# Rotary embedding on one core: tables first, one queue for loads and stores, 2 MB slabs, small first and last pieces, -sin on ScalarE

## Chip, cores, metric

The kernel runs on one NeuronCore of one Trainium2 chip. The metric is the device time of one execution in microseconds (us). "Span" is the length of the profiled execution; it is 1.7 to 1.8 us shorter than the time of the same run.

## The reference

`x` is float32 of shape 8 x 2048 x 8 x 64 (batch, sequence, heads, head size), 33.5 MB; `cos` and `sin` are 2048 x 32, 256 KB each.

```python
def reference(x, cos, sin):
    x1 = x[..., :32]; x2 = x[..., 32:]
    cos = cos[None, :, None, :]; sin = sin[None, :, None, :]
    out1 = x1 * cos - x2 * sin
    out2 = x1 * sin + x2 * cos
    return np.concatenate([out1, out2], axis=-1)
```

Every element is read once and written once, so at least 67 MB move. There are four multiplies and two adds for each pair, all elementwise.

## The kernel before

Each of the 128 partitions holds 16 neighbouring rows of the sequence of every batch, so a partition's data of one batch is 32 KB of contiguous memory. A tile is 4 of these rows (1 MB, 8 KB in each partition); there are 32 tiles and 20 buffers. GpSimd makes the sine products (`t2`), VectorE the cosine product (`t1`, in PSUM) and the sum. Loads are issued on the sync queue, stores and both tables on the ACT queue.

```python
    nc.scalar.dma_start(out=sin_sb, in_=sin_src)
    nc.scalar.dma_start(out=cos_sb, in_=cos_src)
    tiles = [(b, l) for l in range(n_blk) for b in range(B)]
    for i, (b, l) in enumerate(tiles):                      # 32 loads of 1 MB
        xt = xpool.tile([P, FREE], f32, tag="xt", name=f"xt{i}")
        nc.sync.dma_start(out=xt, in_=xv[b, :, l * FREE : (l + 1) * FREE])
        xts.append(xt)
    nc.vector.tensor_scalar_mul(ssin[:, :, 0, :], sin_sb, -1.0)   # -sin, sin
    nc.vector.tensor_copy(ssin[:, :, 1, :], sin_sb)
    nc.vector.tensor_copy(cos_ps, cos_sb)                         # cos to PSUM
    for i, (b, l) in enumerate(tiles):
        # ... (cut: tiles t1 in PSUM, t2 in SBUF, views)
        for u in range(2):
            nc.gpsimd.tensor_mul(out=..., in0=..., in1=rep(ssin[..., u, :], H))
        nc.vector.tensor_mul(out=t1..., in0=xt..., in1=rep(cos_ps[...], 2 * H))
        nc.vector.tensor_add(out=xt, in0=t1, in1=t2)
        nc.scalar.dma_start(out=ov[b, :, l * FREE : (l + 1) * FREE], in_=xt)
```

## Time and profile before

| | before |
|---|---|
| time, median | 168.08 us (3 runs, 168.06 to 168.24) |
| span | 166.6 us |
| VectorE / GpSimd busy | 148.2 / 146.3 us |
| bytes moved | 67.65 MB |
| first work on VectorE's tiles | 10.64 us |
| last add ends | 161.8 us |

From the page of the kernel before: the span, the busy times, the bytes per second in 40 equal slices of the span (4.2 us each), and the chain that ended last, by engine and by line.

```profile
span 166.6 us, 381 instructions
...
DVE 148.2 (89%) x67; POOL 146.3 (88%) x68
...
GB/s 167 424 428 421 374 431 423 433 427 425 431 421 431 429 427 427 425 433 419 433 425 423 433 419 433 423 433 427 425 431 421 431 427 427 429 423 433 285 220 252
...
DVE 89%; DMA 5%; issue 2%; DVEq 0%; ACTq 0%
DVE t L78 44%; DVE xt L83 44%; DMA cos_sb<-in_cos_dram 5%; DVE cos_ps L60 0%; DVEq L83 0%; ACTq L48 0%
```

Three things are nearly level: VectorE and GpSimd are busy for 88 to 89%, and the DMA moves 420 to 430 GB/s in nearly every slice. But the chain names VectorE for 89%, and the rest is the wait for the cosine table at the head; after the first slice and a dip to 374 in the fifth, the DMA slows down only in the last three slices, where it waits for VectorE.

From the timeline of the kernel before (columns: start, duration, engine, line, operation, what it writes and reads, shapes; in brackets the idle time of the engine before it and what ended it):

```profile
6.75 0.43 DVE L58 TENSOR_SCALAR ssin<-sin_sb 128x512 f32<-128x512 f32 x1 [6.75 <-DMA sin_sb<-in_sin_dram]
...
7.25 22.99 POOL L73 TENSOR_TENSOR t<-xt,ssin 128x1024 f32<-128x1024 f32 x10 [6.81 <-DVE ssin L58]
9.91 0.69 DVE L60 COPY cos_ps<-cos_sb 128x512 f32<-128x512 f32 x1 [2.41 <-DMA cos_sb<-in_cos_dram]
10.64 2.29 DVE L78 TENSOR_TENSOR t<-xt,cos_ps 128x2048 f32<-128x2048 f32 x1
13.04 2.29 DVE L83 TENSOR_TENSOR xt<-t,t 128x2048 f32<-128x2048 f32 x1
...
159.52 2.29 DVE L83 TENSOR_TENSOR xt<-t,t 128x2048 f32<-128x2048 f32 x1
```

The tables land at 6.75 and 9.91 us, VectorE begins its tiles at 10.64 and ends at 161.8: 32 pairs of multiply and add at 4.725 us, with no gap. GpSimd, with 64 operations between 7.25 and 153.4, needs 4.57 us a tile: a little faster than VectorE, and it starts 3.4 us ahead.

From the windows of the kernel before (columns: window, its length, VectorE's busy time and operations, GpSimd's the same, granted clock, busy share of the DMA engines, GB/s):

```profile
8.00:60.00 52.00, 48.67 (x22) 52.00 (x24) 1.00 1.01 423
60.00:120.00 60.00, 58.21 (x27) 60.00 (x27) 1.00 1.01 427
...
156.00:160.00 4.00, 3.86 (x3) 0.00 (x0) 1.00 0.70 289
160.00:162.00 2.00, 1.81 (x1) 0.00 (x0) 1.00 0.17 70
162.00:166.00 4.00, 0.00 (x0) 0.00 (x0) 1.00 0.64 262
```

The DMA is saturated (share about 1.0) at 423 to 427 GB/s, and after 156 us it has pauses: it waits for tiles. The tail, from the last add to the end, is 4.8 us and holds a 1 MB store.

### The profile page before, as it was taken

To read this page: it belongs to the slowest core of one execution; us is meant where nothing else is said; L and a number is where in the kernel's file an instruction comes from. 1 tells how busy PE (TensorE), PEld (TensorE's weight loads), DVE (VectorE), ACT (ScalarE), POOL (GpSimd) and SP (SyncE) were. 2 spreads that over 40 slices of the span, in tenths; PEclk is the share of its full clock that TensorE was granted. 3 is DMA by queue.
4 is the path that set the end of the run, shared out by engine and by line. 5 is a ranking of instruction groups with operands and counts; after the bars stand their busy time and mean duration, and the time that the engine had idled before them with its cause. 6 is when DMAs were issued, how large, how long until landed. Compare 5 with 4: busy or idle time off the path is not lost.

```text
span 166.6 us, 381 instructions
## 1 busy us (share of the span) xinstructions
DVE 148.2 (89%) x67; POOL 146.3 (88%) x68
## 2 busy tenths in 40 slices
DVE  0169999999999999999999999999999999999980
POOL 0299999999999999999999999999999999998000
DMA  5999999999999999999999999999999999999656
GB/s 167 424 428 421 374 431 423 433 427 425 431 421 431 429 427 427 425 433 419 433 425 423 433 419 433 423 433 427 425 431 421 431 427 427 429 423 433 285 220 252
DMA packets 9506, 67.65 MB, mean 406 GB/s; under 512 B 1056, under 2 KB 1056, under 8 KB 1312
## 3 DMA queue, kind: packets, MB, share of 16 engines
q10 hardware_dynamic: 4896, 34.08, 48.6%
q1 hardware_dynamic: 4608, 33.56, 48.3%
q14 instruction: 2, 0.02, 0.0%
HBM read 34.08 MB, written 33.55 MB: 406 GB/s over the span
## 4 chain that ended last, share of the span: by engine, by line
DVE 89%; DMA 5%; issue 2%; DVEq 0%; ACTq 0%
DVE t L78 44%; DVE xt L83 44%; DMA cos_sb<-in_cos_dram 5%; DVE cos_ps L60 0%; DVEq L83 0%; ACTq L48 0%
## 5 line engine op out<-in xcount | busy, mean ns | idle before, releaser
L73 POOL TENSOR_TENSOR t<-xt,ssin 128x1024 f32<-128x1024 f32 x64 | 146.1, 2341 | 6.8 <-DVE ssin L58 6.8
L83 DVE TENSOR_TENSOR xt<-t,t 128x2048 f32<-128x2048 f32 x32 | 73.3, 2291 | 3.3
L78 DVE TENSOR_TENSOR t<-xt,cos_ps 128x2048 f32<-128x2048 f32 x32 | 73.5, 2296 | 1.1
L58 DVE TENSOR_SCALAR ssin<-sin_sb 128x512 f32<-128x512 f32 x1 | 0.4, 426 | 6.7 <-DMA sin_sb<-in_sin_dram 6.7
L60 DVE COPY cos_ps<-cos_sb 128x512 f32<-128x512 f32 x1 | 0.7, 694 | 2.4 <-DMA cos_sb<-in_cos_dram 2.4
L59 DVE COPY ssin<-sin_sb 128x512 f32<-128x512 f32 x1 | 0.4, 419 | 0.0
L99 POOL MEMSET const-float32-0.0<- 128x1 f32 x1 | 0.1, 98 | 0.2 <-issue 0.2
L99 POOL MEMSET const-bfloat16-1.0<- 128x1 bf16 x1 | 0.1, 101 | 0.0
L99 POOL MEMSET const-uint8-127<- 128x1 uint8 x1 | 0.1, 101 | 0.0
L99 POOL MEMSET const-float32-1.0<- 128x1 f32 x1 | 0.1, 98 | 0.0
## 6 DMA issues: line engine op xcount, KB each, us to landing
xt<-in_x_dram SPq DMA_DIRECT2D x32, 1024.0 KB, 20.6
out_dram<-xt ACTq DMA_DIRECT2D x32, 1024.0 KB, 10.7
sin_sb<-in_sin_dram ACTq DMA_DIRECT2D x1, 256.0 KB, 6.0
cos_sb<-in_cos_dram ACTq DMA_DIRECT2D x1, 256.0 KB, 8.7
```

Source lines behind the costliest of these rows:

```text
L58: nc.vector.tensor_scalar_mul(ssin[:, :, 0, :], sin_sb, -1.0)
L59: nc.vector.tensor_copy(ssin[:, :, 1, :], sin_sb)
L60: nc.vector.tensor_copy(cos_ps, cos_sb)
L73: nc.gpsimd.tensor_mul(out=dst.rearrange("p (r h) d -> p r h d", h=H), in0=src.rearrange("p (r h) d -> p r h d", h=H), in1=rep(ssin[:, l * ...
L78: nc.vector.tensor_mul(out=t1.rearrange("p (r k d) -> p r k d", r=SL, d=Dh), in0=xt.rearrange("p (r k d) -> p r k d", r=SL, d=Dh), in1=rep ...
L83: nc.vector.tensor_add(out=xt, in0=t1, in1=t2)
L99: nc = _bacc.Bacc("TRN2", target_bir_lowering=False, num_devices=1)
```

## The change

The intent: start earlier (tables first, small first pieces, -sin made by ScalarE, which is idle), end sooner (small last pieces), and let loads and stores run in one orderly queue with large transfers: ten slabs of 2 MB are read ahead, then stores and loads alternate. The diff, cut to its core:

```diff
-    SL = 4                      # 32 tiles of 1 MB, 20 buffers
+    SL = 8                      # 16 slabs of 2 MB, 10 buffers
+    SLAB = SL * HD; UNIT = 4 * HD; NBUF = 10     # UNIT is 1 MB, HD is 256 KB
-    nc.scalar.dma_start(out=sin_sb, in_=sin_src)
+    def cuts(i):                # loads of slab i
+        if i == 0: return [HD, HD, 2 * HD, UNIT]
+        return [SLAB]
+    def pieces(i):              # computation
+        if i == 0: return [HD, HD, 2 * HD, UNIT]
+        if i == last: return [UNIT, 2 * HD, HD, HD]
+        return [UNIT, UNIT]
+    def stores(i): return pieces(i) if i == last else [SLAB]
+    nc.sync.dma_start(out=sin_sb, in_=sin_src)
     nc.scalar.dma_start(out=cos_sb, in_=cos_src)
+    for i in range(NBUF): load(i)                # all on the sync queue
-    nc.vector.tensor_scalar_mul(ssin[:, :, 0, :], sin_sb, -1.0)
-    nc.vector.tensor_copy(ssin[:, :, 1, :], sin_sb)
+    nc.scalar.mul(nsin, sin_sb, -1.0)
     nc.vector.tensor_copy(cos_ps, cos_sb)
     ...
+        for u, tab in ((1, sin_sb), (0, nsin)):  # GpSimd, plain sin first
     ...
+    for i, (b, l) in enumerate(slabs):
+        ...                                      # compute the pieces of slab i;
+                nc.sync.dma_start(out=ov[...], in_=xts[i][...])   # its stores
+        if i >= 1 and i - 1 + NBUF <= last:
+            load(i - 1 + NBUF)                   # into the buffer of slab i - 1
-        nc.scalar.dma_start(out=ov[b, :, l * FREE : (l + 1) * FREE], in_=xt)
```

More of the change, by code (lines that the diff above doesn't have):

```diff
@@ L20 @@
     f32 = mybir.dt.float32
+    PSUM = bass.MemoryType.PSUM
     B, S, H, D = x.shape
@@ L26 @@
     R = S // P
-    SL = 4
-    n_blk = R // SL
-    FREE = SL * HD
+    SL = 8
+    n_half = R // SL
+    SLAB = SL * HD
+    UNIT = 4 * HD
+    NBUF = 10
     xv = x.rearrange("b (q r) h d -> b q (r h d)", q=P)
@@ L37 @@
     const_pool = ctx.enter_context(tc.tile_pool(name="const", bufs=1))
-    cps_pool = ctx.enter_context(tc.tile_pool(name="cps", bufs=1, space=bass.MemoryType.PSUM))
-    t1_pool = ctx.enter_context(tc.tile_pool(name="t1p", bufs=1, space=bass.MemoryType.PSUM))
-    xpool = ctx.enter_context(tc.tile_pool(name="xpool", bufs=20))
+    tab_pool = ctx.enter_context(tc.tile_pool(name="tab", bufs=1, space=PSUM))
+    t1_pool = ctx.enter_context(tc.tile_pool(name="t1p", bufs=1, space=PSUM))
+    xpool = ctx.enter_context(tc.tile_pool(name="xpool", bufs=NBUF))
     t2_pool = ctx.enter_context(tc.tile_pool(name="t2p", bufs=3))
@@ L44, with stores, spans, load @@
     sin_sb = const_pool.tile([P, R, Dh], f32, tag="sb")
-    ssin = const_pool.tile([P, R, 2, Dh], f32, tag="ss")
-    cos_ps = cps_pool.tile([P, R, Dh], f32, tag="cp")
-    nc.scalar.dma_start(out=sin_sb, in_=sin_src)
-    nc.scalar.dma_start(out=cos_sb, in_=cos_src)
-    tiles = [(b, l) for l in range(n_blk) for b in range(B)]
-    xts = []
-    for i, (b, l) in enumerate(tiles):
-        xt = xpool.tile([P, FREE], f32, tag="xt", name=f"xt{i}")
-        nc.sync.dma_start(out=xt, in_=xv[b, :, l * FREE : (l + 1) * FREE])
-        xts.append(xt)
-    nc.vector.tensor_scalar_mul(ssin[:, :, 0, :], sin_sb, -1.0)
-    nc.vector.tensor_copy(ssin[:, :, 1, :], sin_sb)
+    nsin = const_pool.tile([P, R, Dh], f32, tag="ns")
+    cos_ps = tab_pool.tile([P, R, Dh], f32, tag="cp")
+    slabs = [(b, l) for l in range(n_half) for b in range(B)]
+    last = len(slabs) - 1
+    xts = {}
+    def cuts(i):
+        if i == 0:
+            return [HD, HD, 2 * HD, UNIT]
+        return [SLAB]
+    def pieces(i):
+        if i == 0:
+            return [HD, HD, 2 * HD, UNIT]
+        if i == last:
+            return [UNIT, 2 * HD, HD, HD]
+        return [UNIT, UNIT]
+    def stores(i):
+        return pieces(i) if i == last else [SLAB]
+    def spans(sizes):
+        lo = 0
+        for n in sizes:
+            yield lo, n
+            lo += n
+    def load(i):
+        b, l = slabs[i]
+        xt = xpool.tile([P, SLAB], f32, tag="xt", name=f"xt{i}")
+        for lo, n in spans(cuts(i)):
+            nc.sync.dma_start(
+                out=xt[:, lo : lo + n],
+                in_=xv[b, :, l * SLAB + lo : l * SLAB + lo + n],
+            )
+        xts[i] = xt
+    nc.sync.dma_start(out=sin_sb, in_=sin_src)
+    nc.scalar.dma_start(out=cos_sb, in_=cos_src)
+    for i in range(NBUF):
+        load(i)
+    nc.scalar.mul(nsin, sin_sb, -1.0)
     nc.vector.tensor_copy(cos_ps, cos_sb)
@@ L63, in rep, with rotate @@
         return dataclasses.replace(a, ap=[a.ap[0][:], a.ap[1][:], [0, n], a.ap[-1][:]])
-    for i, (b, l) in enumerate(tiles):
-        xt = xts[i]
-        t1 = t1_pool.tile([P, FREE], f32, tag="t1")
-        t2 = t2_pool.tile([P, FREE], f32, tag="t2")
-        for u in range(2):
-            dst = t2.rearrange("p (rh u d) -> p rh u d", u=2, d=Dh)[:, :, u, :]
-            src = xt.rearrange("p (rh u d) -> p rh u d", u=2, d=Dh)[:, :, 1 - u, :]
+    def rotate(i, lo, n):
+        b, l = slabs[i]
+        xt = xts[i][:, lo : lo + n]
+        r0 = l * SL + lo // HD
+        nr = n // HD
+        t1 = t1_pool.tile([P, n], f32, tag="t1")
+        t2 = t2_pool.tile([P, n], f32, tag="t2")
+        xu = xt.rearrange("p (g u d) -> p g u d", u=2, d=Dh)
+        t2u = t2.rearrange("p (g u d) -> p g u d", u=2, d=Dh)
+        for u, tab in ((1, sin_sb), (0, nsin)):
@@ L73 @@
             nc.gpsimd.tensor_mul(
-                out=dst.rearrange("p (r h) d -> p r h d", h=H),
-                in0=src.rearrange("p (r h) d -> p r h d", h=H),
-                in1=rep(ssin[:, l * SL : (l + 1) * SL, u, :], H),
+                out=t2u[:, :, u, :].rearrange("p (r h) d -> p r h d", h=H),
+                in0=xu[:, :, 1 - u, :].rearrange("p (r h) d -> p r h d", h=H),
+                in1=rep(tab[:, r0 : r0 + nr, :], H),
             )
         nc.vector.tensor_mul(
-            out=t1.rearrange("p (r k d) -> p r k d", r=SL, d=Dh),
@@ L80 @@
-            in0=xt.rearrange("p (r k d) -> p r k d", r=SL, d=Dh),
-            in1=rep(cos_ps[:, l * SL : (l + 1) * SL, :], 2 * H),
+            out=t1.rearrange("p (r k d) -> p r k d", r=nr, d=Dh),
+            in0=xt.rearrange("p (r k d) -> p r k d", r=nr, d=Dh),
+            in1=rep(cos_ps[:, r0 : r0 + nr, :], 2 * H),
         )
         nc.vector.tensor_add(out=xt, in0=t1, in1=t2)
-        nc.scalar.dma_start(out=ov[b, :, l * FREE : (l + 1) * FREE], in_=xt)
+    for i, (b, l) in enumerate(slabs):
+        done = 0
+        st = list(spans(stores(i)))
+        for lo, n in spans(pieces(i)):
+            rotate(i, lo, n)
+            done = lo + n
+            while st and st[0][0] + st[0][1] <= done:
+                slo, sn = st.pop(0)
+                nc.sync.dma_start(
+                    out=ov[b, :, l * SLAB + slo : l * SLAB + slo + sn],
+                    in_=xts[i][:, slo : slo + sn],
+                )
+        if i >= 1 and i - 1 + NBUF <= last:
+            load(i - 1 + NBUF)
```

## The prediction

> **What bounds the kernel now.** Three things run level. The chain of waits is VectorE for 89% of the 166.6 us span: from 10.64 to 161.8 us it does one multiply and one add per 1 MB tile every 4.725 us, without a gap (timeline). GpSimd needs 4.57 us per tile (7.25 to 153.4 us). The DMA engines are saturated from 4 to 156 us at about 427 GB/s (windows: busy share 1.01); the Trainium skill, "DMA: Bandwidth & Descriptors", Specifications, gives a ceiling of 435, 2% above this trace. The head is 10.6 us: sin lands at 6.75, cos at 9.9, since their 2 KB packets take turns with 8 KB packets of x (fits a 1:4 share, with 1.2 us from last byte to landing). The tail is 4.8 us: the last 1 MB store.
>
> **Head.** Sin (sync queue) and cos (ACT queue) now meet only 2 KB packets: both should land near 5.0 us (about 0.5 MB moved), the first quarter tile near 5.6. VectorE loses the two sin operations (0.43 + 0.42 us), keeps the cos copy (0.69). GpSimd starts at about 5.7, VectorE at about 5.8. But VectorE then waits for GpSimd, which had a lead of 3.4 us before and has none now: about 2 us of waits within the first four tiles' worth. VectorE ends slab 1 at about 26.8 us; it was at 29.5. Gain 2.7 us, not the 4.8 by which it starts earlier. The Trainium skill, "ScalarE: Activation LUTs", What ACT_TABLE_LOAD costs, gives about 1.3 us for a table load; I expect it to hide behind the wait for sin.
>
> **Middle.** VectorE keeps 4.725 us per half slab: same operations, shapes, memories. One queue instead of two should not change the DMA rate: loads alone (4 to 16 us), stores alone (140 to 156) and the mixture all ran at 424 to 433 GB/s. The queue reads ten slabs (to about 54 us) before a store moves, yet no load is late: slab i lands near 5 + 4.9(i+1), needed near 8 + 9.45i. The transfer queued ahead covers each load's wait for a store.
>
> **Tail.** Slab 15 in four pieces costs VectorE two more pairs of 0.46 us fixed cost (4.725 less 2 x 2048 elements at 1.04 ns, the slope between its 512- and 2048-element operations), 0.9 us; the last add ends near 160.0. The last store is 256 KB: issue 0.34, start 0.8, transfer 0.65, end 1.5: about 3.2 us instead of 4.8. Gain 0.7 us. The DMA backlog (67.65 MB at 427 to 431 GB/s) runs out at about 160 to 161, so it adds little.
>
> **Sum.** Gain 3.4 us: span about 163.2, time about 164.8 us (168.08 before), range 163.6 to 166.4. Faster by over 2%: 0.45; within 2%: 0.53; slower: 0.02.
>
> **Right if:** cos lands near 5 us; VectorE waits 1.5 to 2.5 us for GpSimd before 27 us and hardly after; never for x after slab 1; DMA at 425 to 432 GB/s from 5 to 155 us; last add near 160; under 3.5 us from it to the end.
>
> **Wrong if:** GpSimd's or ScalarE's small operations carry a large fixed cost (it passes straight to the end); the table load comes after sin; the single queue drains at a change between loads and stores (a dip to 328 GB/s stood once, at 18 to 20 us, just after the first store; thirteen of these would cost 5 us); or the last stores queue behind a DMA backlog.

## The result

The changed kernel takes 166.45 us (median of 4 runs, 166.1 to 166.99) where the one before takes 168.16 us (4 runs beside it, 168.06 to 168.39). The ratio is 0.990 (95% interval 0.987 to 0.993): 1% faster. All ratios here are the mean time of one kernel's runs over the mean time of the other's runs in the same rounds, so not quite the ratio of the medians. Executions over 1.5% slower than the fastest of the same kernel are left out of the means. The changed kernel also scatters by 0.9 us, where the one before scatters by 0.3.

From the page of the changed kernel:

```profile
span 164.9 us, 327 instructions
...
DVE 148.8 (90%) x73; ACT 1.9 (1%) x2; POOL 147.6 (90%) x76
...
GB/s 186 309 431 433 437 441 413 429 437 433 417 425 441 433 417 429 421 437 415 429 441 409 431 429 429 433 429 425 425 437 425 429 433 429 437 433 386 429 392 109
...
DVE 83%; DMA 8%; POOL 3%; issue 2%; SPq 1%; DVEq 0%; POOLq 0%
DVE xt L117 42%; DVE t L112 41%; DMA xt<-in_x_dram 8%; POOL t L107 3%; SPq L80 1%; DVEq L117 0%; SPq L86 0%; POOLq L107 0%
```

The span is 1.7 us shorter. The chain is still VectorE's, its share is smaller, and the last slice moves 109 GB/s, although nothing is left to compute in it.

From the timeline of the changed kernel:

```profile
1.16 1.28 ACT L91 ACT_TABLE_LOAD   x1 [1.16 <-PEq L147]
...
4.19 0.69 DVE L92 COPY cos_ps<-cos_sb 128x512 f32<-128x512 f32 x1 [4.19 <-DMA cos_sb<-in_cos_dram]
4.97 0.70 DVE L112 TENSOR_TENSOR t<-xt,cos_ps 128x512 f32<-128x512 f32 x1
5.01 0.72 POOL L107 TENSOR_TENSOR t<-xt,sin_sb 128x256 f32<-128x256 f32 x1 [4.57 <-DMA xt<-in_x_dram]
...
7.30 0.72 POOL L107 TENSOR_TENSOR t<-xt,sin_sb 128x256 f32<-128x256 f32 x1 [0.90 <-DMA xt<-in_x_dram]
...
15.77 2.29 DVE L117 TENSOR_TENSOR xt<-t,t 128x2048 f32<-128x2048 f32 x1 [1.06 <-POOL t L107]
...
20.64 2.29 DVE L117 TENSOR_TENSOR xt<-t,t 128x2048 f32<-128x2048 f32 x1 [0.25 <-POOL t L107]
...
160.11 0.69 DVE L117 TENSOR_TENSOR xt<-t,t 128x512 f32<-128x512 f32 x1
```

The cosine table is there at 4.19 us and VectorE works on x at 4.97, 5.7 us earlier than before. The second quarter of a tile makes GpSimd wait until 7.30, and VectorE waits for GpSimd several times until 20.64. The last add ends at 160.8, only 1.0 us earlier than before. The span ends at 164.9, so the tail is 4.1 us, though the last store has only 256 KB.

From the windows of the changed kernel (columns as before, with ScalarE's busy time between VectorE's and GpSimd's):

```profile
4.00:8.00 4.00, 2.75 (x4) 0.63 (x1) 2.09 (x4) 1.00 0.95 298
29.00:34.00 5.00, 4.86 (x3) 0.00 (x0) 5.00 (x3) 1.00 1.00 426
8.00:60.00 52.00, 48.31 (x24) 0.00 (x0) 51.73 (x26) 1.00 1.01 430
60.00:120.00 60.00, 58.23 (x27) 0.00 (x0) 60.00 (x27) 1.00 1.01 428
...
156.00:160.00 4.00, 3.72 (x5) 0.00 (x0) 0.64 (x1) 1.00 0.95 395
160.00:162.00 2.00, 0.69 (x2) 0.00 (x0) 0.00 (x0) 1.00 0.60 234
162.00:166.00 4.00, 0.00 (x0) 0.00 (x0) 0.00 (x0) 1.00 0.14 53
```

The middle is as fast as before (428 to 430 GB/s). The head, 4 to 8 us, is slow: 298 GB/s at a busy share of 0.95. Between 160 and 162 us the mean engine is busy for only 60% of the time, since the last stores wait for VectorE (experiment 6, without a late landing, has 42% there); after 162 us something still moves.

### Reading the 16 completion steps

A DMA tells its landing by raising a semaphore in 16 steps. The Trainium skill, "DMA: Bandwidth & Descriptors", Why a DMA increments its semaphore by 16 and not by 1, says that each engine that takes part adds its one step after its own data. So the time between the first and the last of the 16 steps shows how far the engines have drifted apart; what follows rests on that reading. I took them from the traces, in us:

| kernel | tenth load: first, last (spread) | a store near 150: first, last (spread) | last store: issue; first, median, last step | end of span |
|---|---|---|---|---|
| before | (1 MB tiles) | 149.40, 150.40 (1.00) | 161.84; 165.54, 165.61, 165.69 | 166.6 |
| changed | 53.73, 55.01 (1.28) | 146.24, 149.32 (3.08) | 160.83; 162.65, 162.75, 164.02 | 164.9 |
| changed, again (experiment) | 53.59, 54.60 (1.01) | 145.97, 149.37 (3.40) | 160.42; 162.25, 162.34, 164.06 | 164.9 |

In the changed kernel one engine, or a few, are 3 us behind the first by 150 us. Of the last store's 16 steps 13 have come by 162.82 us, the others at 163.56, 163.74 and 164.02, and 0.85 us later the span ends. In the first trace the spread of the stores and loads between 65 and 120 us grows only at loads: 1.12 (store, landed at 74.6), 1.85 (load, 80.0), 1.68 (store, 84.8), 2.22 (load, 90.0), and so on to 3.09 (load, 120.2), and then it stays between 3.07 and 3.09 for seven stores, when no load comes any more.

A caution on two queues: while loads and stores share the engines there, the spread of the loads' steps reaches 2.3 us too (kernel before: 2.28 at the load landed at 128.4, but 0.39 at the store landed at 128.6). So engines drift apart with two queues as well. The stores after the last load, near 150 us, are what the comparison rests on.

### The profile page after: what moved, and what is told of

The parts are those of the page before. It is cut to its first block, busy times and chain, and to the rows that moved or that the text cites. A ratio compares the mean times of both kernels' runs of the same rounds, so it can differ in the third digit from the quotient of the medians.

```text
span 164.9 us, 327 instructions
## 1 busy us (share of the span) xinstructions
DVE 148.8 (90%) x73; ACT 1.9 (1%) x2; POOL 147.6 (90%) x76
## 4 chain that ended last, share of the span: by engine, by line
DVE 83%; DMA 8%; POOL 3%; issue 2%; SPq 1%; DVEq 0%; POOLq 0%
DVE xt L117 42%; DVE t L112 41%; DMA xt<-in_x_dram 8%; POOL t L107 3%; SPq L80 1%; DVEq L117 0%; SPq L86 0%; POOLq L107 0%
## 5 line engine op out<-in xcount | busy, mean ns | idle before, releaser
L107 POOL TENSOR_TENSOR t<-xt,sin_sb 128x1024 f32<-128x1024 f32 (+2 forms) x36 | 75.0, 2083 | 8.8 <-DMA xt<-in_x_dram 5.7
L117 DVE TENSOR_TENSOR xt<-t,t 128x2048 f32<-128x2048 f32 (+2 forms) x36 | 73.9, 2054 | 6.4 <-POOL t L107 3.3
L112 DVE TENSOR_TENSOR t<-xt,cos_ps 128x2048 f32<-128x2048 f32 (+2 forms) x36 | 74.1, 2059 | 1.4 <-DMA xt<-in_x_dram 0.2
L107 POOL TENSOR_TENSOR t<-xt,nsin 128x1024 f32<-128x1024 f32 (+2 forms) x36 | 75.0, 2083 | 0.0
L91 ACT ACT_TABLE_LOAD x1 | 1.3, 1283 | 1.2 <-PEq L147 1.2
L91 ACT ACTIVATE nsin<-sin_sb 128x512 f32<-128x512 f32 x1 | 0.6, 630 | 1.6 <-DMA sin_sb<-in_sin_dram 1.6
```

The lines of the kernel that those rows point to most:

```text
L91: nc.scalar.mul(nsin, sin_sb, -1.0)
L107: nc.gpsimd.tensor_mul(out=t2u[:, :, u, :].rearrange("p (r h) d -> p r h d", h=H), in0=xu[:, :, 1 - u, :].rearrange("p (r h) d -> p r h d" ...
L112: nc.vector.tensor_mul(out=t1.rearrange("p (r k d) -> p r k d", r=nr, d=Dh), in0=xt.rearrange("p (r k d) -> p r k d", r=nr, d=Dh), in1=rep ...
```

## Experiments

Theory A (late engine): where one queue goes from a store to a load, some packets of the load take longer, each time on a few engines. All engines are saturated, so an engine that is hit stays late, and the last stores wait for it. Rival B (backlog): the bytes simply aren't through yet, and the queue doesn't matter. Rival C: the head is at fault, with its slow small rows.

### 1. Two queues

```diff
-                nc.sync.dma_start(out=ov[...
+                nc.scalar.dma_start(out=ov[...
```

> The changed kernel with its stores issued on the ACT queue, loads on the sync queue, all else the same. Theory (stalled packets): in the changed kernel a few load packets take 0.4 to 0.9 us too long each time the single queue goes from a store to a load; engines that are all saturated can't catch up, so the 16 completion steps of the last stores are spread over 1.4 to 2.4 us and the last landing is late. With two queues the mixture is made packet by packet, as in the kernel before: hardly any such packet after 65 us, spread of the last stores under 1.2 us, from the last add to the end 3.0 to 3.4 us (4.1 in the changed kernel), ratio to before about 0.982. Rival (backlog): the last stores wait only because 67.65 MB are not through; then the queue doesn't matter, tail 4.0 us or more and ratio 0.988 to 0.992. Also possible: loads slow down once stores begin at 20 us and VectorE waits for x in the middle.

Measured: 164.73 us against 168.18, ratio 0.979 (0.978 to 0.981), span 162.8. The spread near 150 us is 1.11 us, the last add ends at 159.8 and the tail is 3.0 us. That part of A holds which says that the last stores land late in one queue, and B falls. But the head of this trace happened to be faster too (see 7), so this run alone does not say how much of the 1.7 us is the queue's.

### 2. No small pieces at the end

```diff
-            return [UNIT, 2 * HD, HD, HD]
+            return [UNIT, UNIT]
```

> The changed kernel without the small pieces at the end (slab 15 computed and stored as two halves of 1 MB). Theory: the split of the tail gained nothing, since its two extra pairs cost VectorE 0.92 us and the last stores stand behind a DMA backlog with one late engine anyway: last add near 159.9 instead of 160.8, tail 4.8 to 5.2 us, span 164.6 to 165.2, ratio 0.988 to 0.993, the same as the changed kernel. Rival (the prediction's own account, tail split worth 0.7 us): span 165.5 or more, ratio 0.994 or more.

Measured: 166.42 us (165.54 to 166.98), ratio 0.990 (0.989 to 0.992): the small last pieces are worth nothing in the changed kernel, as expected. The profiled execution is the fastest of the five (span 163.7, below the range that I gave); its last add ends at 158.9 and its tail is 4.8 us. The steps of its last store, of 1 MB, lie within 0.15 us, and it takes 3.85 us from issue to landing, as the last 1 MB store of the kernel before does: in this trace the size of the last store sets the end, not a late engine.

### 3. No small pieces at the head

```diff
-            return [HD, HD, 2 * HD, UNIT]     # loads and computation of slab 0
+            return [UNIT, UNIT]
```

> The changed kernel without the small pieces at the head (slab 0 loaded and computed as two halves of 1 MB). Theory (narrow rows stall): the packets of 0.5 to 1 us at 4 to 8.5 us come from rows of 2 and 4 KB taken out of 32 KB of HBM; without them the first half lands near 6.9 us, and slab 1 ends at about 28.0 us on VectorE against 27.7: the small head pieces are worth only 0.3 to 0.5 us; ratio 0.991 to 0.994; few packets over 0.45 us after each engine's first of x. Rival (first touch of x stalls whatever the row width): many 8 KB packets over 0.45 us up to 8 us, first half lands at 7.5 us or later, ratio 0.995 or more.

Measured: 166.32 us (166.30 to 166.35), ratio 0.989 (0.987 to 0.990): not slower at all, while I expected 0.3% or so. The first half lands at 6.72 us, slab 1 ends on VectorE at 27.95, as expected, and the last add ends at 161.5. The tail is 3.0 us: the last store was issued 0.7 us later than in the changed kernel and landed 0.5 us earlier (163.56 against 164.02). So the small first pieces are worth nothing either, and the scatter is gone with them. Two things temper this. VectorE is only 0.3 us later than the changed kernel at slab 1 (27.95 against 27.66); 0.53 us more is a pause between a multiply and its add at 87.5 us that no wait in the trace explains. Experiment 5 has it too (0.51 at 87.4), and experiment 9 (0.52 at 72.0). And the spread near 150 us is 1.77 us here, with one queue as well: the engines drifted less than in the changed kernel, and that isn't explained either.

### 4. The tables alone

The kernel before, with sin first on the sync queue, cos alone on the ACT queue, and -sin by ScalarE; two queues, 1 MB tiles and 20 buffers stay.

```diff
-    nc.scalar.dma_start(out=sin_sb, in_=sin_src)
+    nc.sync.dma_start(out=sin_sb, in_=sin_src)
-    nc.vector.tensor_scalar_mul(ssin[:, :, 0, :], sin_sb, -1.0)
-    nc.vector.tensor_copy(ssin[:, :, 1, :], sin_sb)
+    nc.scalar.mul(nsin, sin_sb, -1.0)
-        for u in range(2):
+        for u, tab in ((1, sin_sb), (0, nsin)):
```

> The kernel before with one part of the change alone: sin first on the sync queue, cos alone on the ACT queue, -sin made by ScalarE, the two sin operations gone from VectorE. Two queues, 1 MB tiles and 20 buffers as before. Theory: cos lands near 4.2 us, the first tile near 7.0; VectorE starts near 7.0, waits about 2.3 us for GpSimd once, last add near 160.5, tail 4.8, span 165.3, ratio 0.992: this alone is three quarters of what the whole change gained (1.3 of 1.7 us). Rival (the gain comes from the one queue, the slabs and the small pieces): ratio 0.997 or more.

Measured: 166.84 us, ratio 0.992 (0.990 to 0.993), span 165.1. From its timeline:

```profile
4.27 0.69 DVE L59 COPY cos_ps<-cos_sb 128x512 f32<-128x512 f32 x1 [4.27 <-DMA cos_sb<-in_cos_dram]
6.82 2.30 DVE L77 TENSOR_TENSOR t<-xt,cos_ps 128x2048 f32<-128x2048 f32 x1 [1.85 <-DMA xt<-in_x_dram]
6.86 2.32 POOL L72 TENSOR_TENSOR t<-xt,sin_sb 128x1024 f32<-128x1024 f32 x1 [6.42 <-DMA xt<-in_x_dram]
...
11.49 2.29 DVE L82 TENSOR_TENSOR xt<-t,t 128x2048 f32<-128x2048 f32 x1 [2.38 <-POOL t L72]
```

The cosine table and the first tile are there when VectorE needs them, then it waits 2.4 us once for GpSimd, which started with it instead of 3.4 us ahead. Slab 1's worth ends at 27.95 us (29.51 before). This one part makes 1.3 us of the whole change's 1.7; the queue, the slabs and the small pieces together make the other 0.4.

### 5. Two queues with the plain head

Experiments 1 and 3 together.

> Stores on the ACT queue and slab 0 in two halves: the third corner of a square (changed 0.990, plain head 0.989, two queues 0.979). Theory: one queue costs time only through the late engine, and only where VectorE is done before that engine; with the plain head VectorE is done at 161.5 us, later than the late engine's backlog, so two queues gain nothing here: last add near 161.5, tail 3.0, ratio 0.987 to 0.990. Rival (one queue makes the DMA slower all along, or costs VectorE time): two queues gain their 1.7 us here too, ratio 0.980 or less.

Measured: 166.27 us (166.23 to 166.28), ratio 0.989 (0.987 to 0.990); last add at 161.5, tail 3.0. This is the corner of the square that separates A from a queue that is slower all along: with the plain head VectorE is done so late that the queue makes no difference (0.9886 with one, 0.9887 with two); with the small first pieces VectorE is done earlier and the queue makes 1.1%. The one queue acts as a second limit at the end of the program, not as a tax on each transfer. The spreads near 150 us were 1.77 (one queue) and 1.45 us (two), closer than with the small pieces, so the square alone doesn't say whether the late VectorE or the smaller drift hid the queue.

### 6. Only the late loads on the other queue

```diff
-            nc.sync.dma_start(
+            (nc.scalar if i >= NBUF else nc.sync).dma_start(      # loads
```

> The changed kernel with only the loads of slabs 10 to 15 on the ACT queue; the first ten loads and all stores stay on the sync queue in their order, and the first store still moves only after ten slabs (near 55 us). Theory (one ring that turns from stores to loads makes some load packets stall, and the saturated engine that they hit stays late): the spread of the stores' completion steps stays under 1.8 us near 150 us (2.0 to 3.4 in five traces with one queue and the same late loads), the last landing comes within 3.3 us of the last add, ratio 0.978 to 0.983. Rival (what helped in the kernel with two queues was that stores begin at 20 us): spread 2 us or more, ratio 0.987 or more.

Measured: 164.63 us (164.25 to 164.83), ratio 0.979 (0.977 to 0.980), span 162.9. This is the closest comparison of all. Head, slabs, small pieces, the order of the stores and the time of the first store (about 55 us) are the changed kernel's; only six loads have left the queue in which they stood behind stores. From its windows, to be held against those of the changed kernel:

```profile
8.00:60.00 52.00, 48.82 (x24) 0.00 (x0) 51.68 (x24) 1.00 1.01 431
60.00:120.00 60.00, 58.27 (x26) 0.00 (x0) 60.00 (x27) 1.00 1.01 430
...
156.00:160.00 4.00, 3.71 (x5) 0.00 (x0) 0.00 (x0) 1.00 0.98 402
160.00:162.00 2.00, 0.00 (x0) 0.00 (x0) 0.00 (x0) 1.00 0.42 158
162.00:166.00 4.00, 0.00 (x0) 0.00 (x0) 0.00 (x0) 1.00 0.00 0
```

The middle is as fast (430 to 431 GB/s), but after 162 us nothing is left to move, where the changed kernel still moves 53 GB/s on average. Two thirds of that, until 162.4 us at 343 GB/s, is the rest of its last store, issued 0.8 us later than here; what follows, 47 GB/s until 164 us, is the work of the late engines. The landing of the last stores shows the same; first the changed kernel, then this one (store, queue, operation, number, size, median us from issue to landing; issues from 154 to 163 us):

```profile
out_dram<-xt SPq DMA_DIRECT2D x1, 1024.0 KB, 6.3
out_dram<-xt SPq DMA_DIRECT2D x1, 512.0 KB, 5.0
out_dram<-xt SPq DMA_DIRECT2D x2, 256.0 KB, 3.6
```

```profile
out_dram<-xt SPq DMA_DIRECT2D x1, 1024.0 KB, 4.6
out_dram<-xt SPq DMA_DIRECT2D x1, 512.0 KB, 3.2
out_dram<-xt SPq DMA_DIRECT2D x2, 256.0 KB, 2.2
```

The 1 MB store lands 4.6 us after its issue instead of 6.3, the 256 KB ones 2.2 instead of 3.6. The spread near 150 us is 0.98, and the last store's 16 steps lie within 0.17 us. The last add ends at 159.98, so the tail is 2.9 us. The median step of the last store comes 1.9 us after its issue in both kernels, so for most engines the end is the same, against B, and only the latest engines differ. Of the 2.0 us between the spans 1.2 are the shorter tail; 0.8 are an earlier last add, as much as a luckier head gave (slab 1 ends at 26.84 against 27.66), but an earlier VectorE alone did not shorten the changed kernel (see 7). A holds, as far as the landing goes; that stores move early, as in experiment 1, isn't needed. One rival is left: in the changed kernel the loads also hold back stores in SyncE's order of issue (the third store is issued at 60.38 us, just after the first late load at 59.95; here at 36.32), so the run doesn't say whether the common DMA queue or this order makes the engines drift.

### 7. The changed kernel again

> The changed kernel once more, unaltered: a second trace, on the chip of the other runs of this call. Theory: its time scatters by up to 1 us (166.1 to 167.0 before), since two parts of it are luck: how long the narrow head rows stall (the second quarter tile landed at 7.24 us in the first trace, 5.72 and 6.30 in the traces of two kernels with the same head) and how late the latest DMA engine is at the end. Expected: ratio 0.988 to 0.991; the spread of the 16 completion steps of the stores near 150 us again 1.7 to 3.2 us; it grows at the landings of loads between 65 and 120 us. If the spread near 150 us is under 1.2 us the theory of the late engine falls.

Measured: 166.42 us (165.87 to 166.98), ratio 0.990 (0.988 to 0.991), span 164.9; spread near 150 us 3.40, more than the range that I gave. Seven traces have the same head; slab 1 ends on VectorE at 26.62, 26.66, 26.68, 26.83, 26.84, 27.24 and 27.66, and the two latest are the two of the changed kernel. The last add ended at 160.8 in the first trace and 160.4 in this one, yet both have the last landing at 164.02 and 164.06 and both spans are 164.9: VectorE was not the last limit, the late engine was. Two traces could agree by chance, but experiments 1 and 6 have the head of the changed kernel too, and all their runs (164.25 to 165.11 us) lie below all ten of the changed kernel (165.87 to 166.99). Rival C falls as the main cause.

### 8. Half as many turns

```diff
-        if i >= 1 and i - 1 + NBUF <= last:
+        if i % 2 and i + NBUF <= last:
             load(i - 1 + NBUF)
+            load(i + NBUF)
```

> The changed kernel with the later loads issued two at a time (store, store, load, load), so that the single queue goes from stores to loads three times instead of six. Theory (load packets stall just after a store): the spread of the completion steps grows at three places instead of six and is near half: from about 1.1 us after the head to 1.7 to 2.4 us near 150 us, where the changed kernel had 3.1 and 3.4; the time falls by 0.3 to 0.9 us, ratio 0.984 to 0.988. Rival (each late load stalls, whatever stands before it): spread near 3.2 us again, ratio 0.989 to 0.991.

Measured: 165.29 us (164.67 to 165.86, and one run at 167.72, which counts as slow), ratio 0.982 (0.980 to 0.985). The time falls, by a little more than expected; but in the profiled run, one of the slower ones, the spread near 150 us is 2.49, a little above my range, and it grows at both loads of a pair (1.03, 1.35, 1.93 at one pair, 1.67, 2.00, 2.48 at the next), not only at the first. The last add of this trace ended at 159.98 and its last landing came at 163.23, both 0.8 us earlier than in the changed kernel's first trace, so the tail is 4.1 us as there. So fewer turns went with a shorter time, and that the turn alone makes the packets late is not shown.

### 9. Narrow rows in the middle

The head is slow from 4 to 8 us (298 GB/s), and I thought that the rows of 2 and 4 KB, taken out of every 32 KB, were the cause. Here slab 5 is loaded in eight such pieces, far from the start.

```diff
+        if i == 5:
+            return [HD] * 8
```

> The changed kernel with slab 5 loaded in eight pieces of 256 KB, 2 KB out of each 32 KB, at about 30 to 36 us, with no effect of a start there. Theory (narrow rows stall): 2 KB packets of 0.3 us and more instead of 0.084, the stretch runs at 220 to 350 GB/s instead of 430, slab 5 lands 1 to 3 us later than the 35.4 us of the changed kernel, and the spread of the completion steps grows by 1 us or more there. Rival (the slow stretch at 4 to 8 us belongs to the start): 2 KB packets of 0.085 us, 380 GB/s or more, slab 5 lands at 35.4 to 36.2 us, spread unchanged near 1.2 us.

From the windows of this kernel (one run, its state unknown; the columns are those of the changed kernel):

```profile
4.00:8.00 4.00, 2.88 (x5) 0.63 (x1) 3.02 (x5) 1.00 1.00 345
29.00:34.00 5.00, 4.77 (x3) 0.00 (x0) 5.00 (x3) 1.00 1.06 390
```

The run took 167.41 us, with a spread of 3.15 us near 150 us and a tail of 5.4 us; no ratio is drawn from it. My theory falls. The narrow rows run at 390 GB/s between 29 and 34 us (the changed kernel has 426 there), the spread stays at 0.38 us there, and the slab lands at 35.0. The head of the same trace is at 345. Narrow rows cost 8%, not 20 to 30%; the rest belongs to the start, and only together with the small pieces, for the plain head (3) runs at 414 GB/s from 4 to 8 us.

### 10. The head's pieces on two queues

```diff
+            q = nc.scalar if k % 2 else nc.sync      # every second piece of slab 0
```

> The changed kernel with every second piece of slab 0 (the second 256 KB and the 1 MB) loaded from the ACT queue. Rival for the slow head (4 to 8 us at 230 to 370 GB/s): a single queue can't keep small packets flowing, since the tables before them came over two queues at 380 to 414 GB/s. If so: no packets of 2 or 4 KB over 0.4 us, 380 GB/s or more from 4 to 8 us. Theory (the narrow rows themselves stall, 2 or 4 KB out of every 32 KB of HBM): packets of 2 and 4 KB over 0.4 us as before and 230 to 370 GB/s, on two queues too. The whole: ratio 0.988 to 0.992.

Measured: 168.45 us, ratio 1.003 (1.001 to 1.004), worse than either theory expected. The third piece landed at 10.1 us and the fourth at 14.0 (8.5 and 11.0 in the first trace of the changed kernel); their steps spread over 3.6 and 4.4 us. That one queue can't keep small packets flowing is refuted: with a second queue the rate from 4 to 8 us was 366 GB/s, under the 380 that this rival needs, and the pieces were complete later. Why small pieces stall in the first 8 us stays open.

### 11 and 12. A better version, wrong and mended

VectorE waits for GpSimd at the head, and GpSimd is idle for about 7 us at the end. So, on two queues and with the plain head, VectorE makes one of GpSimd's two products in the first half slab (from a copy of -sin in PSUM), and GpSimd makes the last 512 KB whole.

```diff
+    nc.scalar.mul(ns_ps, sin_sb[:, :4, :], -1.0)              # -sin in PSUM
+        head = i == 0 and lo == 0
+        tail = i == last and lo + n == SLAB
+            eng = nc.vector if head and u == 0 else nc.gpsimd   # sine products
+            eng = nc.gpsimd if tail else nc.vector              # cosine product
+        (nc.gpsimd if tail else nc.vector).tensor_add(out=xt, in0=t1, in1=t2)
-            return [UNIT, 2 * HD, HD, HD]
+            return [UNIT, 2 * HD, 2 * HD]
```

> A try at a better version: two queues, slab 0 in two halves; in the first half slab VectorE makes one of GpSimd's two products itself (from a copy of -sin that ScalarE writes to PSUM), so it doesn't wait for GpSimd; the last quarter of slab 15 is made whole by GpSimd, which is idle by then. Theory: VectorE's last add falls to about 157.5 to 158.5 us, GpSimd ends near 158, and the DMA becomes the limit: last landing near 160.7, span 161.3 to 162.3, ratio 0.970 to 0.976. If GpSimd's four operations of the last quarter take longer than 8 us, the gain is lost at the end and the ratio is above 0.980.

Measured: 188.9 us, ratio 1.123. From its waits (who waited for whom: us in total, times, longest):

```profile
POOL t L128 <- DMA xt<-in_x_dram: 27.0, 1, 27.0
```

The cosine product of the last piece wrote to a buffer of its own. Nothing but the load of slab 15 held it back, and the build placed it long before its turn in GpSimd's order; there it stopped GpSimd for 27.0 us. This says nothing about the idea. The mended form works in place (`t1 = xt` for that piece), so that it has to follow the two products that read the same data.

> The try at a better version, mended: in the first form GpSimd's cosine product of the last quarter had its own buffer, so nothing kept it behind its place, and it was put some thirty operations too early in GpSimd's order, where it waited 27 us for slab 15. Now it is made in place, after the two sine products that read the same data. Theory as before: slab 1 ends on VectorE at about 26.8 us, VectorE's last add near 157.0, GpSimd ends near 158.3, last landing near 161, span 161.5 to 162.5, ratio 0.971 to 0.977; GpSimd's order ends with the four operations of the last quarter. If the DMA is the limit sooner than thought, the last stores land after 162 and the ratio stays at 0.979, as with two queues alone.

Measured: 164.29 us (164.25 to 164.69), ratio 0.978 (0.977 to 0.979), span 162.5. Its last operations:

```profile
155.78 1.22 DVE L133 TENSOR_TENSOR xt<-t,t 128x1024 f32<-128x1024 f32 x1
156.44 2.34 POOL L133 TENSOR_TENSOR xt<-xt,t 128x1024 f32<-128x1024 f32 x1
```

VectorE is done at 157.0 us, 3.8 us earlier than in the changed kernel's first trace, GpSimd at 158.8. But the last landing is at 161.4, and the ratio is just above my range. The limit is now GpSimd with its last store: that store, of 512 KB, is issued at 158.81 us, its steps lie within 0.18 us, and just before its packets start the DMA runs dry (191 GB/s from 159.0 to 159.6 us), so no backlog held it; the DMA, at 401 GB/s and more until 159 us, is close behind. It is the fastest version that ran, by a hair: its interval overlaps those of experiments 1 and 6, which change one line of the changed kernel.

## Why the prediction was wrong

The prediction was 164.8 us with a range of 163.6 to 166.4; measured were 166.45, 1.65 us more than predicted. That the number came out just above the range is partly luck: five of the changed kernel's ten runs (experiment 7 included) lie below it.

- **What bounds the kernel before, and the pace of VectorE:** right. The middle kept 4.725 us per half slab, there was no wait for x after slab 1, and the DMA stayed at 428 to 430 GB/s.
- **Head:** the mechanism was right, the size a little off and subject to luck: VectorE started on x at 4.97 (predicted 5.8) and then waited longer, and the two errors nearly cancel. Cos landed at 4.19 (predicted near 5), VectorE waited 3.3 us for GpSimd (predicted 1.5 to 2.5), slab 1 ended at 27.66 and 27.24 in the changed kernel's traces, and the median of all seven traces with this head is 26.83 (predicted 26.8). The smallest GpSimd operations took 0.72 us, more than a quarter (0.58) of a large one's 2.32.
- **"One queue instead of two should not change the DMA rate":** true of the rate, and still the step that failed. I took an unchanged rate to mean unchanged landings. The engines drift apart in one queue (spread 3.1 and 3.4 us near 150 us against 1.0 with the late loads on another queue, experiment 6), at loads that follow stores. Over all traces but that of experiment 11, the spread near 150 us is 1.8 to 3.4 us with late loads and stores in one queue (the changed kernel twice, experiments 2, 3, 8, 9 and 10) and 1.0 to 1.5 us with two queues (the kernel before, experiments 1, 4, 5, 6 and 12).
- **"The DMA backlog ... runs out at about 160 to 161, so it adds little":** this is the mis-sized term. It holds for the median engine only. The tail was put at 3.2 us; it was 4.1 and 4.5. With the late loads on the other queue it was 2.9, the last add at 159.98 (predicted 160.0) and the span 162.9 (predicted 163.2): without this one effect the sum comes out. The prediction had named it under "Wrong if" ("the last stores queue behind a DMA backlog"), and gave it no size.
- **Tail:** the two extra pairs did cost VectorE about 0.9 us, as predicted (last add at 158.9 in experiment 2, 159.98 in 6, with heads 0.2 us apart), but the 0.7 us of net gain did not show (experiment 2), since in the changed kernel the late engine, not the last store's size, sets the end.
- **ScalarE:** right. The table load took 1.28 us (the Trainium skill, "ScalarE: Activation LUTs", What ACT_TABLE_LOAD costs, gives 1283 ns) and ended at 2.44 us, before sin had landed.

What is shown: that putting the late loads in the stores' queue costs the changed kernel about 1.1%; that it does so through the landing of the last stores on the latest engines; that moving six loads to the other queue removes it. Whether the DMA queue or the order of issue at SyncE is at work was not tested. What was only read from traces: that particular packets of the loads are the origin. Packets that took over 40 ns longer than is usual for their size, after 25 us, sum to 8.1 us in the changed kernel and to 0.7 in experiment 1, but to 3.7 in experiment 6 and 23.2 in experiment 3, so their sum over all engines doesn't follow the time; which engine they hit does matter, and the trace doesn't name it. In the kernel before such packets sum to 0.8 us, and its loads still spread to 2.3 us, so they are not the only origin of drift. Why a load behind a store stalls, in one queue, stays open.

## What to carry to other kernels

While the DMA stayed saturated here, the engines that had fallen behind did not catch up: the changed kernel's 3.1 us of spread at 120 us were still there at 154, and 1.4 us at the last store. Where the queue ran empty before the last store, they were gone (0.15 and 0.17 us, experiments 2 and 3). So look at the spread of a transfer's completion steps and not only at GB/s. Before you credit a change of several parts, run the parts: here the tables (their order and queues, with -sin on ScalarE) gave three quarters of the gain, and the small pieces at both ends gave nothing as long as another limit stood behind them. Two engines and the DMA were level here, and each gain at one end soon uncovered the next limit.

## What the Trainium skill lacked or had wrong

- "DMA: Bandwidth & Descriptors", Issuing engines are not separate DMA queues, says that issuing from several engines only saves the sequencer's issue time. The rate agrees (428 and 430 GB/s from 60 to 120 us with one and two queues, experiment 6), the conclusion doesn't: six of the loads on another queue took the ratio from 0.990 to 0.979, since the last stores landed earlier.
- The same page doesn't say that engines drift apart under saturation and fall into step again where the queue runs empty: spread 3.08 us near 150 us in the changed kernel, and 0.15 to 0.18 us at last stores that had little or nothing queued in front of them (kernel before, experiments 2, 3, 5, 6 and 12). With two queues the drift was smaller, 1.0 to 1.5 us near 150 us.
- The same page's Specifications give an HBM limit of about 358 GB/s per core, without saying there that this is a core's share while both cores of its pair stream; the page says so under Bandwidth, where a core alone has 425 GB/s. This program runs on one core and moved 423 to 431 GB/s to and from HBM for over 140 us. The fabric ceiling of 435 in the same table agrees.
- No page that I read explains the first 8 us: with small first pieces the rate from 4 to 8 us was 298 to 375 GB/s in seven traces, narrow rows ran at 390 GB/s in mid-program, and with wide rows it was 414 GB/s at the start.
